# Layer 1's gates and branch projections with tokens on the output partitions and 512 moving weight columns

## The chip, the cores and the metric

One core of a Trainium2 chip runs the kernel. The engines named below are TensorE (PE in the profile; its weight loads are PEld), VectorE (DVE), ScalarE (ACT), GpSimd (POOL) and SyncE (SP, which issues the DMAs of the weights). The metric is the device time of one execution in microseconds; lower is better.

## The reference, cut to what matters

Two layers of a diffusion backbone work on 256 latent tokens and 256 context tokens with 1024 channels. Each layer projects the normalised tokens `h` once; three mixers (latent attention "mla", grouped attention "gqa", a Fourier mixing "four") work side by side. Their outputs, 512 wide each, are projected to 1024 channels, gated and summed, and the sum goes through one more projection:

```python
proj = h @ lp["w_in"]
o_mla = blocked_attend(q_mla, ..., MLA_QK ** -0.5)
o_gqa = blocked_attend(q_gqa, ..., GQA_DIM ** -0.5)
o_four = fourier_mix(proj[..., FOUR_START:GATE_START])
...
g_mla, g_gqa, g_four = jnp.split(jax.nn.sigmoid(gate_cols), N_BRANCH, axis=-1)
y = (g_mla * (o_mla.reshape(b, l, MLA_HEADS * MLA_V) @ lp["w_br_mla"])
     + g_gqa * (o_gqa.reshape(b, l, GQA_HEADS * GQA_DIM) @ lp["w_br_gqa"])
     + g_four * (o_four @ lp["w_four"]))
return y @ lp["w_o"]
```

Here `gate_cols` are the last 3 x 1024 columns of `proj`. A gated feed-forward layer with a short convolution follows. In the second layer (layer 1, `last` in the kernel) only the 256 latent tokens go on behind the keys and values.

## The kernel before

All data are 32 bit floats. A product of two such matrices is made of three matmuls on numbers split into a high and a low part: `mm3` (line 108) adds hi·hi, hi·lo and lo·hi (lines 109, 110 and 111 in the profile). `split` (line 120) makes the parts: ACT writes the high one (line 123, or 125 with a scale), DVE the low one (129 or 131). Weights come by `wchunk` (line 80): one DMA of 512 KB on SP's queue fills a raw tile of 128 x 1024 (three buffers), which is split into one of three high and one of three low buffers.

Activations lie channel major: a tile has 128 channels on the partitions and the tokens along the free side (256 in layer 1, `TQ`). `hs` are the eight normalised tiles of `h` (tags H0 to H7), `os` the four tiles of one mixer's output. `fm_group` (line 413) multiplies weights by them: a 128x128 block of the weight is stationary, the 256 tokens move, and the output has channels on the partitions. Two blocks of 128 output channels share one PSUM bank of 512 columns.

`merge` (line 579) makes, for one branch, two functions. `gate(mc)` takes 256 gate columns of `w_in` (two chunks of 4 k x 256), runs 2 x 8 x 3 = 48 matmuls of 256 columns and lets ACT write tanh of half the result, 128x512 (line 595). `branch(mc)` takes 256 columns of the branch weight (one chunk), runs 2 x 4 x 3 = 24 matmuls, and DVE multiplies the result by the gate plus one (602 for the first branch, straight into the sum `yT`; 604 for the others, whose result POOL adds to the sum, 605). There are three branches: 2 (four: `gF`, `bF`), 1 (gqa: `gG`, `bG`) and 0 (mla: `gM`, `bM`), each with `mc` from 0 to 3. The sum `yT` holds eight channel-major pieces in two tiles (tags Y0, Y1).

Where these run in layer 1: the list `fillers` gives one item behind each head of the gqa loop (lines 890 to 907): `gF` and `bF` of one mc behind each of heads 0 to 3, then the mla key and query tokens, then `gG(0)` and `gG(1)`. `bG(0)` and `gG(2)` stand between the two loops. The list `plan` gives the items behind the eight heads of the mla loop (945 to 960): `bG(1)`, `bG(2)`, `gG(3)`, `bG(3)`, then `gM(0)` to `gM(3)`. `heads_kq` (928) transposes one head's keys into the one bank of tag "tk" and its queries into a bank of tag "mm", a head ahead. Behind the loop stand the four `bM`, in banks of "s" and "mm" by turns, then the split of the eight pieces of the sum (line 972, tiles `yh` in H0 to H7), and the output projection `o` (lines 993 to 1016), with the first two chunks of 256 columns in two halves of k: 0 to 5, then 6 and 7.

PSUM has banks of tags "mm" (2), "s" (2, the scores of attention), "pt" (2, transposed probabilities), "o" (1) and "tk" (1). The order of the instructions on each engine is set at build time by a scheduler that takes the program's order as priority and a model of the times; within it, a filler's matmuls slip in between those of the heads.

## Time and profile before

| | us |
|---|---|
| median of 3 runs | 1373.64 (1371.73 to 1374.29) |
| the profiled execution, its own time | 1373.26 |
| its span in the profile | 1371.5 |
| PE busy in it | 1334.1 (97%) |
| DVE, ACT, POOL busy | 949.2, 660.1, 335.0 |

The profile is of one execution. Its span runs from the first to the last instruction; the execution's own time holds 1.8 us more. Layer 1's three mixers with gates and branches lie between about 955 us and 1145 us of the span: the gqa loop until about 1018, the hand-over with the mla keys and queries until about 1057, the mla loop until about 1126, and then the last branch, the sum and the start of the output projection. The shown durations of matmuls overlap, as they are pipelined and their ends are modelled; how fast they follow one another is read from their starts in the timeline.

### The profile page before, as it was taken

To read this page: it belongs to the slowest core of one execution; us is meant where nothing else is said; L and a number is where in the kernel's file an instruction comes from. 1 tells how busy PE (TensorE), PEld (TensorE's weight loads), DVE (VectorE), ACT (ScalarE), POOL (GpSimd) and SP (SyncE) were. 2 spreads that over 40 slices of the span, in tenths; PEclk is the share of its full clock that TensorE was granted. 3 is DMA by queue.
4 is the path that set the end of the run, shared out by engine and by line. 5 is a ranking of instruction groups with operands and counts; after the bars stand their busy time and mean duration, and the time that the engine had idled before them with its cause. 6 is when DMAs were issued, how large, how long until landed. Compare 5 with 4: busy or idle time off the path is not lost.

```text
span 1371.5 us, 22227 instructions
## 1 busy us (share of the span) xinstructions
PE 1334.1 (97%) x8381; PEld 1168.4 (85%) x8381; DVE 949.2 (69%) x1686; ACT 660.1 (48%) x1166; POOL 335.0 (24%) x399
## 2 busy tenths in 40 slices
PE   7999999999999899999999999999998999999998
PEld 4887888877888788888788888898988999899998
DVE  4675665676656647777876776777788867888853
ACT  4434555434556235434213443455665664666642
POOL 2211222365322421011000111222244524112200
PEclk8999999999999999999999999999999999999999
DMA  9733452243323524334674445634424366466663
GB/s 322 255 95 117 131 168 62 62 113 102 104 73 110 202 69 132 120 111 138 185 234 130 142 146 182 194 108 120 128 74 146 93 187 204 138 182 184 186 188 119
DMA packets 160437, 197.40 MB, mean 144 GB/s; under 512 B 7080, under 2 KB 144858, under 8 KB 160330
## 3 DMA queue, kind: packets, MB, share of 16 engines
q1 hardware_dynamic: 159328, 195.32, 46.1%
q8 instruction: 66, 1.08, 0.3%
q0 software_dynamic: 864, 0.61, 0.3%
q14 instruction: 41, 0.34, 0.1%
q10 hardware_dynamic: 138, 0.04, 0.0%
HBM read 191.76 MB, written 3.15 MB: 142 GB/s over the span
## 4 chain that ended last, share of the span: by engine, by line
PE 89%; DVE 6%; DMA 2%; POOL 1%; issue 1%; ACT 1%; SPq 0%; ACTq 0%; DVEq 0%; POOLq 0%
PE L0upp L109 6%; PE L0upp L110 6%; PE L0upp L111 6%; PE L1upp L109 3%; PE L1upp L110 3%; PE L1upp L111 3%; PE L0dp L109 3%; PE L0dp L111 3%; PE L0dp L110 3%; PE L0gp L109 3%; PE L0gp L111 3%; PE L0gp L110 3%; PE L1dp L111 2%; PE L1dp L110 2%; PE L1dp L109 2%; PE L0bp L111 1%
## 5 line engine op out<-in xcount | busy, mean ns | idle before, releaser
L109 PE MATMUL L0upp<-L0n_h,L0up_h 128*128 128x512 f32 (+1 forms) x384 | 141.5, 372 | 1.1 <-ACT L0n_h L377 1.1
L110 PE MATMUL L0upp<-L0n_h,L0up_h 128*128 128x512 f32 (+1 forms) x384 | 142.5, 373 | 0.0
L111 PE MATMUL L0upp<-L0n_h,L0up_l 128*128 128x512 f32 (+1 forms) x384 | 139.1, 371 | 0.0
L1079 POOL TENSOR_TENSOR L0sg<-L0sg,L0u 128x512 f32<-128x512 f32 x22 | 29.6, 1345 | 274.1 <-DVE L0u L1056 274.1
L109 PE MATMUL L1upp<-L1n_h,L1up_h 128*128 128x256 f32 x352 | 95.4, 283 | 1.1 <-ACT L1n_h L377 1.1
L111 PE MATMUL L1upp<-L1n_h,L1up_l 128*128 128x256 f32 x352 | 96.1, 283 | 0.0
L110 PE MATMUL L1upp<-L1n_h,L1up_h 128*128 128x256 f32 x352 | 95.8, 283 | 0.0
L109 PEld LDWEIGHTS L0upp<-L0n_h,L0up_h 128*128 128x128 f32 x384 | 71.9, 188 | 14.3 <-ACT L0n_h L377 1.5
L110 PEld LDWEIGHTS L0upp<-L0n_h,L0up_h 128*128 128x128 f32 x384 | 72.2, 188 | 13.0 <-DVE L0n_t L376 0.4
L111 PEld LDWEIGHTS L0upp<-L0n_h,L0up_l 128*128 128x128 f32 x384 | 72.2, 188 | 12.5
L123 ACT CAST L0up_h<-L0up_w 128x1024 fp32r<-128x1024 f32 x44 | 46.4, 1054 | 74.6 <-PE L0upp L110 51.2
L129 DVE TENSOR_TENSOR L0up_l<-L0up_w,L0up_h 128x1024 fp32r<-128x1024 f32 x44 | 59.2, 1348 | 32.1 <-ACT L0up_h L123 31.6
L109 PE MATMUL L0gp<-L0n_h,L0g_h 128*128 128x512 f32 x192 | 75.9, 396 | 1.1 <-ACT L0gt L594 1.1
L110 PE MATMUL L0gp<-L0n_h,L0g_h 128*128 128x512 f32 x192 | 75.7, 394 | 0.0
L111 PE MATMUL L0gp<-L0n_h,L0g_l 128*128 128x512 f32 x192 | 75.1, 396 | 0.1
L299 DVE SCALAR_TENSOR_TENSOR mod_acc<-mod_w,cpad,mod_acc 128x1024 f32<-128x1024 f32 x49 | 62.4, 1297 | 15.8 <-DMA mod_w<-in_w_mod_dram 15.8
L109 PE MATMUL L0dp<-L0act,L0dn_h 128*128 128x512 f32 (+1 forms) x196 | 72.8, 372 | 0.0
L111 PE MATMUL L0dp<-L0act,L0dn_l 128*128 128x512 f32 (+1 forms) x196 | 72.4, 370 | 0.0
L110 PE MATMUL L0dp<-L0act,L0dn_h 128*128 128x512 f32 (+1 forms) x196 | 72.2, 368 | 0.0
L109 PEld LDWEIGHTS L1upp<-L1n_h,L1up_h 128*128 128x128 f32 x352 | 65.9, 192 | 1.5 <-ACT L1n_h L377 1.5
L111 PEld LDWEIGHTS L1upp<-L1n_h,L1up_l 128*128 128x128 f32 x352 | 66.4, 192 | 0.0
L110 PEld LDWEIGHTS L1upp<-L1n_h,L1up_h 128*128 128x128 f32 x352 | 66.2, 192 | 0.1
(1564 smaller groups left out, 4265.2 us busy)
## 6 DMA issues: line engine op xcount, KB each, us to landing
mod_w<-in_w_mod_dram SPq DMA_DIRECT2D x96, 512.0 KB, 5.0
L0up_w<-in_w_up_dram SPq DMA_DIRECT2D x44, 512.0 KB, 3.6
L1up_w<-in_w_up_dram SPq DMA_DIRECT2D x44, 512.0 KB, 4.3
L0g_w<-in_w_in_dram SPq DMA_DIRECT2D x24, 512.0 KB, 3.7
L1g_w<-in_w_in_dram SPq DMA_DIRECT2D x24, 512.0 KB, 3.7
L0dn_w<-in_w_down_dram SPq DMA_DIRECT2D x20, 512.0 KB, 4.0
L1dn_w<-in_w_down_dram SPq DMA_DIRECT2D x16, 512.0 KB, 3.6
L0wo_w<-in_w_o_dram SPq DMA_DIRECT2D x8, 512.0 KB, 3.4
```

What stands on the lines that cost most here:

```text
L109: nc.tensor.matmul(ps, lh, rh, start=start, stop=False)
L110: nc.tensor.matmul(ps, lh, rl, start=False, stop=False)
L111: last_mm[0] = nc.tensor.matmul(ps, ll, rh, start=False, stop=stop).ins
L123: nc.scalar.copy(hi, src)
L129: ins = nc.vector.tensor_sub(lo, src, f(hi))
L299: nc.vector.scalar_tensor_tensor(acc, raw, cv, acc, op0=ALU.mult, op1=ALU.add)
L1079: nc.gpsimd.tensor_mul(g[:, :TQ], g[:, :TQ], us[1][:, :TQ])
```

## The change

In layer 1, `merge` returns the two functions of a new `merge_tokens`. Stationary is now a block of 128 tokens of `hs` or `os` (the high or the low part), and 512 columns of the weight move over it; the output has tokens on the partitions and one of two halves c of the channels along the free side. Both token tiles (tt) of a half have a PSUM bank of 512 columns each. A gate half takes four chunks of 2 k x 512 and 8 x 2 x 3 = 48 matmuls; it can be made in parts of one or two chunks, the banks being held between them. A branch half takes two chunks and 24 matmuls. Layer 0 keeps its `merge`.

The sum is kept token major, 128 x 1024 for each token tile. The adds of branch 0 go from POOL to DVE. `turn_sum(c)` transposes half c of the sum into four channel-major pieces in banks of tag "pt", and splits two pieces at a time (tiles in H4 to H7). The first half is turned between the two chunks of the last branch half, the second in the output projection, whose halves of k are now 0 to 3 and 4 to 7. The lists change: `fillers` have `gF(0)`, `bF(0)`, `gF(1)`, `bF(1)`, the key and query tokens, and `gG(0)` in two parts; `bG(0)` uses the "s" banks; a half of `gG(1)` stands ahead of the mla loop; `plan` has the other half of `gG(1)`, `bG(1)`, and `gM(0)` in parts of 1, 2, 1 chunks and `gM(1)` in parts of 2, 1, 1. The queries of an mla head are transposed into the "tk" bank, as the keys are.

```diff
--- before.py
+++ after.py
@@ -467,8 +467,7 @@
         run_after(mods["n1"], before)
         if last:
 
-            ytiles = [S.tile([P, 4, 256], F32, tag=f"Y{i}", name=f"{n_}y{i}") for i in range(2)]
-            yT = [ytiles[m // 4][:, m % 4, :] for m in range(KD)]
+            ytiles = [S.tile([P, D], F32, tag=f"Y{i}", name=f"{n_}y{i}") for i in range(2)]
             xk = [S.tile([P, 4, 256], F32, tag=f"Y{2 + i}", name=f"{n_}xk{i}") for i in range(2)]
             for m in range(KD):
                 nc.sync.dma_start(out=xk[m // 4][:, m % 4, :], in_=xT[m][:, :256])
@@ -576,14 +575,62 @@
             rope_apply(nc.vector, qg[tt], qg[tt], "qg", tt, H, 64, f"{n_}qgr{tt}")
 
 
+        def merge_tokens(b, wname, os, first):
+
+
+            begun, gates = {}, {}
+
+            def products(ps, w, xs, k0, nk):
+                for tt in range(2):
+                    ts = slice(tt * P, (tt + 1) * P)
+                    for k in (k0, k0 + 1):
+                        wh, wl = w(k - k0, 0, 512)
+                        mm3(ps[tt], xs[k][:, 0, ts], xs[k][:, 1, ts], wh, wl, k == 0, k == nk - 1)
+
+            def gate(c, n=4, tag=None):
+                i0, pss = begun.get(c) or (0, [pm(f"{n_}gp{b}{c}{tt}") for tt in range(2)])
+                for i in range(i0, i0 + n):
+                    w = wchunk(w_in, 2 * i, 2, GATE_START + b * D + c * 512, 512, f"{n_}g{b}{c}{i}")
+                    products(pss, w, hs, 2 * i, KD)
+                begun[c] = i0 + n, pss
+                if i0 + n < 4:
+                    return
+                if tag:
+                    t = S.tile([P, 2, 512], F32, tag=tag, name=f"{n_}gt{b}{c}")
+                    gates[c] = [t[:, tt] for tt in range(2)]
+                else:
+                    gates[c] = [S.tile([P, 512], F32, tag="gate", name=f"{n_}gt{b}{c}{tt}", bufs=3) for tt in range(2)]
+                for tt in range(2):
+                    nc.scalar.activation(gates[c][tt], pss[tt], AF.Tanh, scale=0.5)
+
+            def branch(c, pieces=(0, 1), bank="mm", own=None):
+                if pieces[0] == 0:
+                    begun[c] = 4, [pm(f"{n_}bp{b}{c}{tt}", bank) for tt in range(2)]
+                pss = begun[c][1]
+                for i in pieces:
+                    w = wchunk(a[wname][l], 2 * i, 2, c * 512, 512, f"{n_}b{b}{c}{i}", own)
+                    products(pss, w, os, 2 * i, 4)
+                if pieces[-1] == 0:
+                    return
+                for tt in range(2):
+                    y, g = ytiles[tt][:, c * 512:(c + 1) * 512], gates[c][tt]
+                    if first:
+                        nc.vector.scalar_tensor_tensor(y, g, 1.0, pss[tt], op0=ALU.add, op1=ALU.mult)
+                    else:
+                        nc.vector.scalar_tensor_tensor(g, g, 1.0, pss[tt], op0=ALU.add, op1=ALU.mult)
+                        (nc.gpsimd if b else nc.vector).tensor_add(y, y, g)
+            return gate, branch
+
         def merge(b, wname, os, first, bank="mm"):
+            if last:
+                return merge_tokens(b, wname, os, first)
             gates, packed = {}, {}
 
             def gate(mc, tag=None, halves=(0, 1)):
                 if 0 in halves:
-                    if tag or last:
-                        pool, nb = (wpool, 2) if tag == "mraw" else (S, None if tag else 3)
-                        t = pool.tile([P, 512 if not tag else 1024], F32, tag=tag or "gate", name=f"{n_}gt{b}{mc}", bufs=nb)
+                    if tag:
+                        pool, nb = (wpool, 2) if tag == "mraw" else (S, None)
+                        t = pool.tile([P, 1024], F32, tag=tag, name=f"{n_}gt{b}{mc}", bufs=nb)
                         packed[mc] = t[:, :2 * TQ]
                         gates[mc] = [t[:, i * TQ:(i + 1) * TQ] for i in range(2)]
                     else:
@@ -844,8 +891,8 @@
 
         if last:
             latents()
-            fillers = [[lambda mc=mc: gF(mc), lambda mc=mc: bF(mc)] for mc in range(4)]
-            fillers += [[kv_tokens], [q_tokens], [lambda: gG(0)], [lambda: gG(1)]]
+            fillers = [[lambda c=c, g=g: g(c)] for c in range(2) for g in (gF, bF)]
+            fillers += [[kv_tokens], [q_tokens], [lambda: gG(0, 2)], [lambda: gG(0, 2)]]
         else:
             fillers = [[lambda mc=mc, g=g: g(mc)] for mc in range(4) for g in (gF, bF)]
         fillers = [mods["g"][i:i + 1] + x for i, x in enumerate(fillers)]
@@ -916,10 +963,12 @@
         ktok, qtok, VM = L["ktok"], L["qtok"], L["VM"]
 
         gM, bM = merge(0, "w_br_mla", om, False, "s")
-        bG(0)
         if last:
-            plan = [[(bG, 1)], [(bG, 2)], [(gG, 3)], [(bG, 3)], [(gM, 0)], [(gM, 1)], [(gM, 2)], [(gM, 3, "D4")], []]
+            bG(0, bank="s")
+            plan = [[(gG, 1, 2)], [(bG, 1)], [(gM, 0, 1)], [(gM, 0, 2)], [(gM, 0, 1)], [(gM, 1, 2)], [(gM, 1, 1)],
+                    [(gM, 1, 1, "D4")], []]
         else:
+            bG(0)
             plan = [[(bG, 1)], [(gG, 2), (bG, 2)], [(gG, 3), (bG, 3)], [],
                     [(gM, 1, "X3")], [(gM, 2, "mraw")], [(gM, 3, "mraw")], [], [(gM, 0)]]
         plan = [[lambda x=x: x[0](*x[1:]) for x in xs] for xs in plan]
@@ -932,14 +981,14 @@
                 nc.tensor.transpose(tk[:96, tt * P:(tt + 1) * P], ktok[tt][:, h, :], ident)
             k2 = pair(f"D{h % 2}", f"{nm}k")
             split(tk[:96, :], k2[:96, 0, :], k2[:96, 1, :], p["gk"])
-            tq = pm(f"{nm}tq", "mm" if last else "tk")
+            tq = pm(f"{nm}tq", "tk")
             for tt in range(NTQ):
                 nc.tensor.transpose(tq[:96, tt * P:(tt + 1) * P], qtok[tt][:, h, :], ident)
             q2 = pair(f"D{2 + h % 2}", f"{nm}q")
             split(tq[:96, :TQ], q2[:96, 0, :TQ], q2[:96, 1, :TQ], p["gq"])
             return k2, q2
 
-        gG(2 if last else 1)
+        gG(1, 2) if last else gG(1)
         with tc.issue_after(last_mm[0]):
             kq = heads_kq(0)
         for h in range(H):
@@ -959,19 +1008,35 @@
                 om.append(finish_pair(of, h // 2, 1, f"{nm}om"))
             run(mods["m"][h:h + 1] + plan[h])
         run(plan[8])
-        for mc in range(4):
-            bM(mc, ("s", "mm", "pt", "s")[mc] if not last else ("s", "mm")[mc % 2],
-               [("H0", "H1")] if mc == 3 and not last else None)
-
-        cw = conv_params(l)
-
-
         ys = []
-        for m in range(KD):
-            y = pair(f"H{m}" if last else f"{'BD'[m // 4]}{m % 4}", f"{n_}yh{m}")
-            split(yT[m], y[:, 0, :TQ], y[:, 1, :TQ], 0.5)
-            ys.append(y)
-        if not last:
+
+        def turn_sum(c):
+
+            for j in range(2):
+                ps = pm(f"{n_}yt{c}{j}", "pt")
+                for i in range(2):
+                    m = 4 * c + 2 * j + i
+                    for tt in range(2):
+                        nc.tensor.transpose(ps[:, i * 256 + tt * P:i * 256 + (tt + 1) * P], ytiles[tt][:, m * P:(m + 1) * P], ident)
+                y = pair(f"H{4 + 2 * c + j}", f"{n_}yh{c}{j}")
+                split(ps, y[:, 0, :], y[:, 1, :], 0.5)
+                ys.extend(y[:, :, i * 256:(i + 1) * 256] for i in range(2))
+
+
+        if last:
+            bM(0, bank="s")
+            bM(1, (0,))
+            turn_sum(0)
+            bM(1, (1,))
+            cw = conv_params(l)
+        else:
+            for mc in range(4):
+                bM(mc, ("s", "mm", "pt", "s")[mc], [("H0", "H1")] if mc == 3 else None)
+            cw = conv_params(l)
+            for m in range(KD):
+                y = pair(f"{'BD'[m // 4]}{m % 4}", f"{n_}yh{m}")
+                split(yT[m], y[:, 0, :], y[:, 1, :], 0.5)
+                ys.append(y)
             xt = [S.tile([P, 2, 512], F32, tag=f"X{i}", name=f"{n_}x{i}") for i in range(4)]
             xn = [xt[m // 2][:, m % 2, :] for m in range(KD)]
             for m in range(KD):
@@ -995,8 +1060,11 @@
             wos.append(wchunk(a["w_o"][l], 0, KD, mc * 256, 256, f"{n_}wo{mc}",
                               None if last else ([("H2", "H3"), ("H4", "H5")], [("H6", "H7"), None])[mc]))
             pos.append([pm(f"{n_}o{mc}_{i}", ("mm", "s")[mc]) for i in range(2)])
-        for ks in (range(6), range(6, KD)):
+        k1 = 4 if last else 6
+        for ks in (range(k1), range(k1, KD)):
             for mc in range(2):
+                if last and ks[0] == 0 and mc == 1:
+                    turn_sum(1)
                 for k in ks:
                     for i in range(2):
                         wh, wl = wos[mc](k, i * P, P)
```

## Rows read from the trace of the kernel before

**Rows 1.** The page: busy time by engine; the chain that ended last, by engine.

```profile
PE 1334.1 (97%) x8381; PEld 1168.4 (85%) x8381; DVE 949.2 (69%) x1686; ACT 660.1 (48%) x1166; POOL 335.0 (24%) x399
...
PE 89%; DVE 6%; DMA 2%; POOL 1%; issue 1%; ACT 1%; SPq 0%; ACTq 0%; DVEq 0%; POOLq 0%
```

**Rows 2.** Busy time in two stretches: by engine; clock, DMA share, GB/s.

```profile
1018.00:1057.00 39.00, 34.46 (x245) 31.34 (x243) 34.05 (x68) 22.12 (x39) 20.87 (x24) 1.00 0.47 135
...
1057.00:1126.00 69.00, 68.48 (x535) 65.75 (x536) 51.84 (x89) 45.63 (x90) 25.97 (x23) 1.00 0.47 138
```

**Rows 3.** Layer 1's gate products: durations ns, first and last start.

```profile
L109 PE MATMUL L1gp<-L1n_h,L1g_h x192: 277/283/387, 955.9 to 1125.0; 128*128 128x256 f32 x192
```

**Rows 4.** The timeline of PE, gate products: start us, shown duration us.

```profile
962.03 0.28 PE L110 MATMUL L1gp<-L1n_h,L1g_h 128*128 128x256 f32 x1
...
963.23 0.28 PE L111 MATMUL L1gp<-L1n_h,L1g_l 128*128 128x256 f32 x1
```

**Rows 5.** The timeline of PE: the Fourier projection's start and end.

```profile
916.52 0.40 PE L109 MATMUL L1fp<-L1fo_h,L1n_h 128*128 128x512 f32 x1
...
927.43 0.28 PE L109 MATMUL L1A<-dft1d,L1f 128*128 128x256 f32 x1
```

**Rows 6.** The timeline of PE: scores of mla head 3, values of head 2.

```profile
1082.48 0.39 PE L110 MATMUL L1m3s<-L1m3k,L1m3q 96*128 96x512 f32 x1
...
1083.41 0.39 PE L111 MATMUL L1m3s<-L1m3k,L1m3q 96*128 96x512 f32 x1
...
1083.99 0.36 PE L693 MATMUL L1m2o<-L1m2ph,L1VM 128*128 128x256 f32 x1
```

**Rows 7.** The timeline of PE: four transposes in the mla loop.

```profile
1081.00 0.60 PE L684 MATMUL L1m2pt<-ident,L1m2p 128*128 128x128 f32 x4
...
1081.56 0.28 PE L111 MATMUL L1gp<-L1n_h,L1g_l 128*128 128x256 f32 x1
```

**Rows 8.** Evictions of gates and branches, the adds, the small low parts.

```profile
L595 ACT ACTIVATE L1gt<-L1gp x12: 589/598/602, 964.4 to 1127.0; 128x512 f32<-128x512 f32 x12
...
L604 DVE SCALAR_TENSOR_TENSOR L1gt<-L1gt,L1bp x8: 668/674/689, 1061.7 to 1144.4; 128x512 f32<-128x512 f32 x8
...
L605 POOL TENSOR_TENSOR L1y<-L1y,L1gt x8: 1281/1348/2367, 1062.5 to 1145.2; 128x512 f32<-128x512 f32 x8
...
L131 DVE SCALAR_TENSOR_TENSOR L1yh<-L1y,L1yh x8: 406/411/1510, 1139.2 to 1148.6; 128x256 fp32r<-128x256 f32 x8
```

**Rows 9.** Low parts on DVE of 128x512 and of a weight chunk.

```profile
L129 DVE TENSOR_TENSOR L1m7ph<-L1m7pt,L1m7ph x2: 681/682/684, 1128.1 to 1128.7; 128x512 fp32r<-128x512 f32 x2
...
L129 DVE TENSOR_TENSOR L1wo_l<-L1wo_w,L1wo_h x8: 1210/1226/2301, 1138.0 to 1160.5; 128x1024 fp32r<-128x1024 f32 x8
```

**Rows 10.** The timeline of PE at the end of the stage.

```profile
1131.92 0.62 PE L109 MATMUL L1bp<-L1m5om,L1b_h 128*128 128x256 f32 x3 [1.35 <-ACT L1m5om L713]
...
1140.42 0.36 PE L109 MATMUL L1o<-L1yh,L1wo_h 128*128 128x256 f32 x1
...
1145.36 0.28 PE L110 MATMUL L1o<-L1yh,L1wo_h 128*128 128x256 f32 x1
```

**Rows 11.** The last mla head: its scores; its output's high and low part.

```profile
L111 PE MATMUL L1m7s<-L1m7k,L1m7q x2: 397/439/481, 1117.3 to 1118.3; 96*128 96x512 f32 x2
...
1131.46 0.40 ACT L713 CAST L1m5om<-L1m6of 128x256 fp32r<-128x256 f32 x1 [0.49 <-DVE L1m6of L698]
...
1131.89 0.43 DVE L714 TENSOR_TENSOR L1m5om<-L1m6of,L1m5om 128x256 fp32r<-128x256 f32 x1 [0.47 <-ACT L1m5om L713]
```

**Rows 12.** Waits of PE from 955 to 1145 us: total, times, longest.

```profile
PE L1gp L109 <- ACT L1gt L595: 0.8, 1, 0.8
...
PE L1m0s L109 <- ACT L1m0q L125: 1.0, 1, 1.0
```

**Rows 13.** The timeline at the first mla head: queries, the key's low part.

```profile
1056.15 0.40 PE L937 MATMUL L1m0tq<-ident,L1qtok 128*96 128x128 f32 x2
...
1057.11 0.74 DVE L131 SCALAR_TENSOR_TENSOR L1m0k<-L1m0tk,gk,L1m0k 96x512 fp32r<-96x512 f32 x1
```

## The prediction

> **What bounds the kernel now.** I read the page first: TensorE (PE) is busy 97% of the 1371.5 us span, and the chain that ended last runs over PE for 89% of it [rows 1]. So a change counts mostly by the time that it takes out of PE's stream, plus what it does to the places where PE stands. Then I read the stretch that the change touches, about 955 to 1145 us, by windows: at the two attention loops PE is nearly solid (68.48 of 69 us between 1057 and 1126), while between 1018 and 1057 it is busy 34.46 of 39 us with VectorE (DVE) busy 34.05; TensorE's granted clock is 1.00 in both, the 2.4 GHz level [rows 2]. So two thirds of the stretch is PE bound, and the hand-over from one attention to the other is held by DVE and ScalarE (ACT) in part.
>
> Busy time hides the rate of the matmuls, as their shown durations overlap (283 ns each for 256 columns, [rows 3]). The rate is the distance from start to start, in the timeline. Gate products of 256 columns start every 0.120 us: from 962.03 to 963.23 there are ten steps [rows 4]. The only place in layer 1 that already works like the changed code (stationary tokens, 512 moving weight columns) is the Fourier projection: 48 matmuls from 916.52 to the start of the next kind at 927.43, 10.91 us or 0.2273 us each [rows 5]. Two of 256 columns cost 0.240, one of 512 costs 0.2273: each instruction carries some 13 ns beside its columns. That 13 ns is what the change is after.
>
> **The change part by part.** *The products.* Before: 12 gates of 48 matmuls and 12 branch blocks of 24, so 864 of 256 columns (each of the three gate lines has 192, [rows 3]); 864 x 0.120 = 103.7 us. After: 6 gates of 8 k x 2 token tiles x 3 = 48, and 6 branches of 24, so 432 of 512 columns; 432 x 0.2273 = 98.2 us. Saved: 5.5 us. The bound on the worse side is the slowest row of 512 columns, the scores of the second attention, with four steps in 0.93 us, 0.2325 each [rows 6]: 100.4 us, 3.3 saved. No row of 512 columns is faster than the Fourier ones, so 5.5 is the better end too.
>
> The Trainium skill, "TensorE: Matmul & The Clock Gate", section "Back-to-back issue gap", gives a gap of N/2.4 + 2.5 ns, which speaks against this change: 109.2 and 215.8 ns, so an estimate of 1.1 us saved, not 5.5. The timeline shows 120 and 227 [rows 4, 5], a fixed part about five times as large; the sum goes by the rows.
>
> The weight loads fall from 864 to 432 too, and the same skill ("Perfetto Trace Analysis", section "Identifying the Most-Contended Engine") judges TensorE's headroom by the busy share of the loads, 85% here [rows 1]. By that one would hope for more: 432 loads at 1168.4 / 8381 = 0.139 us are 60 us. But the two steps differ by 107 ns for 256 columns, just the columns' own time at 2.4 GHz; so the loads lie under the columns, and only the 13 ns are to be had.
>
> *Transposes added.* 16 of 128x128, in four groups of four. Four such in the attention run from 1081.00, and the second matmul behind them starts at 1081.56: 0.56 less the one normal step of 0.12 is 0.44 us a group [rows 7]. 4 x 0.44 = 1.8 us on PE; from 1.3 (the shown 0.60 less the 0.28 of one matmul) to 2.2 (all of the 0.56).
>
> *Evictions, splits and loads.* Gate tanh: 12 of 128x512 before and after, 598 ns each. Branch eviction on DVE: 12 of 128x512 both times, 674 to 688 ns. The splits of weight chunks are 24 + 12 both times (a chunk is 2 k x 512 in place of 4 k x 256), and so are the loads in SP's queue, with rows twice as long in DRAM; hidden under the products, as now: costed at nothing. The adds of the second attention's branch leave POOL (1348 ns each, four of them) for DVE; the trace has no such add on DVE, so I bound it by the lo of 128x512 (682 ns) and by the 128x1024 lo (1226 ns) and take the first, which has its size [rows 8, 9]. The eight small splits of the sum (0.41 us on each of ACT and DVE) become four of 128x512 from PSUM, 0.6 and 0.68: 0.6 us less on each.
>
> *The end of the stage.* Now PE waits 1.35 us for the last attention output, and then the output projection starts in a stutter: 18 matmuls take from 1140.42 to 1145.36, 4.94 us where 18 x 0.120 = 2.2, so 2.8 us are lost to halves of the sum that are not split yet [rows 10]. After the change, from the moment t at which the last output is there: branch half 0 lacks one k (6 matmuls, 1.4 us), then two evictions (1.4) and two adds (1.4) on DVE, four transposes (0.44), ACT's hi (0.6), DVE's lo (0.68), with hops of 0.03 (ACT's 1131.46 + 0.40 to DVE's 1131.89, [rows 11]) and PE's latency twice (0.28 shown less 0.12 of step, 0.16): the output projection can run from about t + 6.3. Cover on PE: 1.4 us of half 0, 2.7 of half 1, 0.9 of transposes, 5.0 in all. A hole of 1.3 us, against 2.8 before. Later DVE owes 2.8 for half 1, 1.4 for two lo, and four weight splits of 1.23; PE has 48 x 0.120 = 5.8 us of first-half products before it needs the second half, so I see no second hole. Change: -1.5 us, from -2.8 (no hole) to +2 (weight splits queued ahead on DVE). The 1.35 us ahead of t [rows 10] I leave as it is: the chain from the last head's last score (1118.3) to its lo (1131.9 + 0.43) took 14 us [rows 11], and the work that can lie beside it (two quarter gates 5.4, three k of half 0 4.1, two k of half 1 2.7, the head's own 1.9) is 14.1.
>
> *Banks.* A channel-major group sat in one PSUM bank and the next group took the other. A token-major group holds both "mm" banks until its tanh or its eviction is done, so PE cannot start the next group meanwhile. It is covered by the stagger: token tile 0 ends six matmuls (1.36 us) ahead of tile 1, and the 0.60 us tanh fits into that; the branch's 0.67 on DVE fits less surely. The nearest row is PE's wait for a gate's tanh, 0.8 us once [rows 12]. With some ten hand-overs I take one such wait, +1.0; from nothing to +4 (half of them). One quarter-gate pair (1.6 us more PE work than before) moves ahead of the second attention, where PE has 4.5 us idle [rows 2]; if it falls into those gaps, 1.6 us more is gained, which I leave to the lower end.
>
> *The q transposes* of each head move from an "mm" bank to the single "tk" bank, behind the k transposes: they now wait until DVE has read k's bank. What is queued behind them on PE are that head's scores, which ACT and DVE then wait for. At the first head q was transposed at 1056.15, while k's bank was read until 1057.11 + 0.74 [rows 13]: up to 1.7 us later, and PE waits there already (1.0 us for q, [rows 12]). From 0 to +1.7; I take +0.5, as half a gate's products stand ready beside it. In the loop k and q are made a head ahead, so it costs nothing there.
>
> *Sum*: -5.5 + 1.8 - 1.5 + 1.0 + 0.5 = -3.7 us. The profiled run took 1373.26 us (span 1371.5), 0.4 under the median of 1373.64 and inside the runs' spread; 1373.26 - 3.7 = **1369.6 us**.
>
> **Rivals.** (a) *The holes close*: larger pieces of work stand ready for PE, so the hole ahead of the output projection goes (-1.3 more), the moved quarter gates fill the hand-over (-1.6) and the q term is nothing (-0.5): 1366.2. For it: PE's idle 4.5 us; against: it is DVE that is busy there. (b) *The pairs of banks eat it*: +4 in place of +1.0, 1372.6. For it: 0.8 us rows exist; against: the stagger. (c) *Slower, by short fillers*: heads 2, 4, 6 and 7 of the second attention now have a quarter gate each, 2.7 us, where most had a whole group of 5.8. Then a head's own 4.0 us on PE (scores 1.4, eight transposes 0.9, eight products with the values 1.0, k and q 0.7) plus 2.7 is 6.7 us, while the chain of its max, exp, POOL product, transposes, split and products took 14 us for the last head [rows 11]; 8.4 us if six tenths of that is its own work and the rest queues, an estimate. If heads ran strictly one behind the other, PE would stand 1.7 us in each of the four, and as long again ahead of t, where the 1.35 us would double: +6.8 + 1.4, 1377.8. It decides when a head overlaps the next by less than 1.7 us. Against it: the scores of head 3 start over 1.5 us ahead of head 2's products with the values (1082.48 and 1083.99, [rows 6]), and the transposes of later heads lie earlier still. (d) *The change doesn't do what it says*: in the loops, with the other engines' traffic beside it, a product of 512 columns takes nearly as long as two of 256, as the scores' 0.2325 goes half the way to [rows 6]; 1.1 us saved in place of 5.5, 1374.0. The Fourier rows stand against it [rows 5]. (The gap rule of the page named above would end at the same time.)
>
> **How the numbers follow.** Forecast 0.47 (1367.7 to 1371.7), (a) 0.15, (b) 0.22, (c) 0.13, (d) 0.03. A measurement of this kernel can tell about 0.2% from no change, 2.7 us: faster means under 1370.9, slower over 1376.4. Four fifths of the forecast's own range lies under 1370.9 (0.38), with (a) 0.53 for faster; the rest of the forecast with (b) and (d), 0.34, is the same; (c), 0.13, is slower. The unknowns alone reach from 1364.7 (-5.5 + 1.3 - 2.8 - 1.6) to 1379.9 (-3.3 + 2.2 + 2 + 4 + 1.7); the range 1365.0 to 1375.5 leaves out (c) and a thin part of (a).
>
> **What the profile after would show.** Steps of 0.227 us for gates and branches of layer 1 (right), or 0.232 and more (the size is off). Four transposes a group at 0.44 us, with PE's idle time ahead of the output projection near 1.3 us in one piece. Waits of PE for gate tanh or branch evictions at more than two hand-overs would show (b); repeated waits of 1.5 us for a head's exp, split or q in the second attention (c). Wrong altogether would be a stretch from the Fourier stage to the feed-forward that is as long as before with steps of 0.227: then work moved into DVE's queue sets the length.

## The result and the profile after

The changed kernel takes 1386.67 us (median of 5 runs, 1386.27 to 1387.02), the kernel before 1373.64 (5 runs, 1371.73 to 1374.87): a ratio of 1.0098, 95% interval 1.0085 to 1.0112. That is 13.0 us slower, where 1369.6 was forecast and 1375.5 was the upper end of the range. The profiled execution (1386.27) has a span of 1384.5 us, again 13.0 more.

The page of the changed kernel, busy time and chain:

```profile
PE 1338.2 (97%) x7965; PEld 1151.2 (83%) x7965; DVE 947.2 (68%) x1686; ACT 658.7 (48%) x1162; POOL 328.5 (24%) x395
...
PE 86%; DVE 6%; DMA 3%; ACT 2%; POOL 2%; issue 1%; SPq 0%; DVEq 0%; ACTq 0%; POOLq 0%
```

Beside [rows 1], PE has 416 matmuls fewer (432 products less, 16 transposes more) and still 4 us more of busy time. The busy share is 97% both times, so it doesn't show the loss.

The lines of the changed kernel (duration ns min/median/max, first and last start), and after "..." the first feed-forward products:

```profile
L109 PE MATMUL L1gp<-L1g_h,L1n_h x96: 387/389/486, 956.2 to 1098.6; 128*128 128x512 f32 x96
...
L1020 PE MATMUL L1yt<-ident,L1y x16: 272/273/421, 1146.3 to 1158.3; 128*128 128x128 f32 x16
...
L621 DVE TENSOR_TENSOR L1y<-L1y,L1gt x4: 679/680/682, 1145.5 to 1150.9; 128x512 f32<-128x512 f32 x4
...
L109 PE MATMUL L1upp<-L1n_h,L1up_h x352: 278/283/415, 1186.3 to 1314.4; 128*128 128x256 f32 x176
```

The same feed-forward line of the kernel before:

```profile
L109 PE MATMUL L1upp<-L1n_h,L1up_h x352: 274/283/387, 1174.8 to 1301.4; 128*128 128x256 f32 x176
```

From the first gate product to the first feed-forward product ("the stage" from here on) the kernel before takes 1174.8 - 955.9 = 218.9 us [rows 3], the changed one 1186.3 - 956.2 = 230.1: 11.2 of the 13.0 us are lost there. And the last gate product starts at 1099, where it was 1125: gate work ran out 41 us before the last attention step, where it used to last nearly to its end.

The windows of the changed kernel (us; PE, PEld, DVE, ACT, POOL busy; granted clock, DMA share, GB/s):

```profile
1018.00:1057.00 39.00, 36.34 (x181) 30.27 (x179) 33.74 (x63) 21.54 (x34) 21.35 (x24) 1.00 0.52 162
1057.00:1126.00 69.00, 64.46 (x337) 52.68 (x338) 50.26 (x81) 43.32 (x83) 22.59 (x19) 0.98 0.39 118
...
1100.00:1108.00 8.00, 5.66 (x32) 4.40 (x31) 5.78 (x11) 5.28 (x12) 1.30 (x2) 1.00 0.42 133
1108.00:1115.00 7.00, 6.36 (x30) 4.82 (x30) 3.93 (x9) 3.63 (x9) 1.41 (x2) 0.76 0.00 0
1115.00:1141.00 26.00, 21.80 (x124) 17.13 (x122) 15.78 (x32) 14.97 (x33) 9.90 (x12) 1.00 0.36 118
1141.00:1150.00 9.00, 5.08 (x26) 3.75 (x26) 6.56 (x11) 3.48 (x5) 1.02 (x2) 1.00 0.73 256
1150.00:1157.00 7.00, 4.92 (x24) 4.76 (x24) 3.25 (x7) 0.60 (x1) 0.00 (x0) 0.52 0.46 150
...
1185.00:1192.00 7.00, 5.89 (x34) 5.58 (x34) 5.86 (x14) 4.52 (x10) 0.74 (x1) 0.76 0.00 0
```

The hand-over became fuller (36.34 of 39 us against 34.46 in [rows 2]), as rival (a) had it. Behind 1100 it is the opposite. The kernel before was solid there at first:

```profile
1100.00:1108.00 8.00, 8.00 (x68) 7.99 (x67) 4.99 (x9) 5.25 (x11) 2.27 (x3) 1.00 0.34 96
```

In the changed kernel PE stands 2.3 us of the first 8, 4.2 of the 26 behind 1115, 3.9 of the 9 behind 1141. And the granted clock, 1.00 all through this stage in the kernel before, falls three times: 0.76 of 7 us, 0.52 of 7 us, 0.76 of 7 us. In shorter windows these are stretches of 3.4, 6.8 and 3.4 us at 0.50, the 1.2 GHz level. Ahead of each PE had stood a good part of the time (5.66 us busy of 8, 5.08 of 9, and 5.38 of 7.5 ahead of the third).

So the account of the stage is: products -5.0 and transposes +1.8 (below); PE's idle time, summed over its gaps, 18.4 us against 10.4, so +8.0; clock 0.24 x 7 + 0.48 x 7 = +5.1, an estimate that takes PE to be the limit while the clock is low. Together that is +9.9 of the 11.2; the other 1.3 us has no place in it. The third clock stretch, 1.7 us, lies in the feed-forward, behind the stage.

Waits of PE in the changed kernel from 1060 to 1182 us (total, times, longest):

```profile
PE L1yt L1020 <- DVE L1y L621: 2.6, 2, 1.3
PE L1o L110 <- DVE L1yh L131: 2.1, 1, 2.1
PE L1bp L109 <- ACT L1m5om L760: 2.0, 2, 1.4
PE L1m4tq L986 <- DVE L1m3st L727: 1.1, 1, 1.1
PE L1m7tq L986 <- DVE L1m6st L727: 1.1, 1, 1.1
PE L1m4s L109 <- ACT L1m4q L125: 0.7, 1, 0.7
```

Two things are on this list that the waits of the kernel before don't have: the q transposes of later heads (L986) wait for DVE, and the transposes of the sum wait twice for an add. The wait for a low part of the sum is 2.1 us in one piece, where the kernel before has two shorter ones:

```profile
PE L1o L110 <- DVE L1yh L131: 1.5, 2, 1.1
```

Nothing waits for a gate's tanh, here or earlier in the stage. The timeline of the changed kernel at head 4 shows the first:

```profile
1103.60 0.60 PE L981 MATMUL L1m4tk<-ident,L1ktok 128*96 128x128 f32 x4
...
1104.54 1.29 DVE L724 TENSOR_REDUCE L1m3st<-L1m3s 128x1 f32<-128x512 f32 x2 [0.59 <-PE L1m3s L111]
...
1105.75 0.74 DVE L131 SCALAR_TENSOR_TENSOR L1m4k<-L1m4tk,gk,L1m4k 96x512 fp32r<-96x512 f32 x1
...
1106.63 0.39 PE L986 MATMUL L1m4tq<-ident,L1qtok 128*96 128x128 f32 x2 [1.13 <-DVE L1m3st L727]
...
1107.71 0.50 PE L109 MATMUL L1m4s<-L1m4k,L1m4q 96*128 96x512 f32 x1 [0.69 <-ACT L1m4q L125]
```

The keys of head 4 are transposed at 1103.60, but DVE's order, set at build time, has the two maxima of head 3 first (1104.54 + 1.29), and DVE reads the keys' bank from 1105.75 to 1106.49. Only then may q go into the same bank: PE stands 1.13 us, then 0.69 more for q's high part, 1.8 us in all ahead of the scores that DVE and ACT need next. (The profile names DVE's last reciprocal as the releaser; what PE needs is the read of the bank that ended at 1106.49.)

### The profile page after: what moved, and what is told of

Its sections match the earlier page's. It is cut to its first block, busy times and chain, and to the rows that moved or that the text cites. A ratio compares the mean times of both kernels' runs of the same rounds, so it can differ in the third digit from the quotient of the medians.

```text
span 1384.5 us, 21368 instructions
## 1 busy us (share of the span) xinstructions
PE 1338.2 (97%) x7965; PEld 1151.2 (83%) x7965; DVE 947.2 (68%) x1686; ACT 658.7 (48%) x1162; POOL 328.5 (24%) x395
## 3 DMA queue, kind: packets, MB, share of 16 engines
q8 instruction: 63, 1.03, 0.3%
## 4 chain that ended last, share of the span: by engine, by line
PE 86%; DVE 6%; DMA 3%; ACT 2%; POOL 2%; issue 1%; SPq 0%; DVEq 0%; ACTq 0%; POOLq 0%
PE L0upp L109 6%; PE L0upp L110 6%; PE L0upp L111 6%; PE L1upp L109 3%; PE L1upp L110 3%; PE L1upp L111 3%; PE L0gp L109 3%; PE L0gp L111 3%; PE L0gp L110 3%; PE L0dp L109 2%; PE L0dp L111 2%; PE L0dp L110 2%; PE L1dp L111 2%; PE L1dp L109 2%; PE L1dp L110 2%; PE L0bp L111 1%
## 5 line engine op out<-in xcount | busy, mean ns | idle before, releaser
L111 PE MATMUL L0upp<-L0n_h,L0up_l 128*128 128x512 f32 (+1 forms) x384 | 139.1, 371 | 0.0
L111 PE MATMUL L1upp<-L1n_h,L1up_l 128*128 128x256 f32 x352 | 97.1, 285 | 0.0
L111 PEld LDWEIGHTS L0upp<-L0n_h,L0up_l 128*128 128x128 f32 x384 | 72.2, 188 | 12.5
L129 DVE TENSOR_TENSOR L0up_l<-L0up_w,L0up_h 128x1024 fp32r<-128x1024 f32 x44 | 59.2, 1347 | 32.1 <-ACT L0up_h L123 31.5
L111 PE MATMUL L0gp<-L0n_h,L0g_l 128*128 128x512 f32 x192 | 75.1, 396 | 0.0
L111 PE MATMUL L0dp<-L0act,L0dn_l 128*128 128x512 f32 (+1 forms) x196 | 72.4, 369 | 0.0
L111 PEld LDWEIGHTS L1upp<-L1n_h,L1up_l 128*128 128x128 f32 x352 | 67.3, 194 | 0.0
```

Of the source, the lines that this page charges most:

```text
L111: last_mm[0] = nc.tensor.matmul(ps, ll, rh, start=False, stop=stop).ins
L129: ins = nc.vector.tensor_sub(lo, src, f(hi))
```

## The experiments

For each: the median (lowest to highest), the ratio to the runs of the kernel before on the same chip (whose medians were 1373.3 to 1374.0), and from its profile the stage, the time from the last gate product to the last attention step ("bare"), and the time lost at the lower clock ("clock": one less the granted clock, summed over windows of 3.5 us from 950 to 1195). The last three columns are of one execution each. All that lies ahead of the stage has the same source in all these kernels, and yet the stage starts between 951.7 us (e3_no_turn) and 958.5 us (e6_before_tk) in the profiled executions. Single executions differ by such amounts for reasons that the edits don't touch, so a difference of two medians is read beside that of the stage.

| kernel | us | ratio (95%) | stage | bare | clock |
|---|---|---|---|---|---|
| before | 1373.64 | | 218.9 | 4.6 | 0 |
| after | 1386.67 | 1.0098 (1.0085 to 1.0112) | 230.1 | 41.2 | 6.8 |
| e2_tq_pt | 1379.24 (1376.67 to 1380.58) | 1.0037 (1.0024 to 1.0050) | 225.6 | 31.9 | 6.8 |
| e6_before_tk | 1385.52 (1384.74 to 1387.03) | 1.0081 (1.0063 to 1.0100) | 227.9 | 20.1 | 1.7 |
| e10_before_tk_pin | 1380.21 (1378.71 to 1381.99) | 1.0048 (1.0032 to 1.0065) | 225.9 | 5.1 | 1.7 |
| e11_before_pt | 1376.66 (1372.68 to 1379.55) | 1.0021 (1.0010 to 1.0032) | 222.1 | 11.4 | 0 |
| e4_early_gates | 1379.84 (1377.88 to 1380.38) | 1.0039 (1.0026 to 1.0052) | 223.6 | 20.1 | 0 |
| e7_before_tk_early | 1390.46 (1389.39 to 1390.75) | 1.0115 (1.0097 to 1.0132) | 233.7 | 28.5 | 5.1 |
| e1_pin | 1385.09 (1383.55 to 1388.68) | 1.0082 (1.0057 to 1.0107) | 231.2 | 11.2 | 8.5 |
| e5_pin_pt | 1382.62 (1381.32 to 1383.79) | 1.0059 (1.0040 to 1.0078) | 226.0 | 11.2 | 6.9 |
| e3_no_turn | 1384.23 (1379.74 to 1385.53) | 1.0068 (1.0046 to 1.0090) | 229.6 | 41.7 | 6.8 |
| e8_tail | 1376.09 (1372.97 to 1377.81) | 1.0016 (1.0005 to 1.0028) | 220.9 | 31.5 | 3.4 |
| e9_spread | 1381.26 (1373.99 to 1383.80) | 1.0048 (1.0032 to 1.0064) | 225.2 | 9.2 | 6.9 |
| e12_fill | 1376.98 (1374.96 to 1379.71) | 1.0026 (1.0016 to 1.0036) | 221.4 | 8.7 | 3.4 |

### The bank of the queries

*e2_tq_pt*, the changed kernel with q in another bank:

```diff
-            tq = pm(f"{nm}tq", "tk")
+            tq = pm(f"{nm}tq", "pt" if last else "tk")
```

> Changed kernel, with the q transposes of the mla heads in a bank of tag pt in place of tk. Theory B (the one tk bank holds up the heads): waits of 1.13, 1.06, 0.69 and 0.61 us for q and its bank go, 3 to 5 us, about 1382 to 1384. Theory A (no filler left): same within 2 us, as the chain of a head stays as long; it may also lose, as pt is taken from the probabilities.

It came out at 1379.24, 7.4 us faster than the changed kernel, more than theory B's 3 to 5; the stage is 4.5 us shorter. Its waits of PE from 1060 to 1182 hold none for tq any more; the first two are those of the stage's end:

```profile
PE L1yt L1020 <- DVE L1y L621: 2.3, 2, 1.6
PE L1o L110 <- DVE L1yh L131: 1.5, 1, 1.5
```

By the medians the bank is over half of the loss, and the mla loop (first scores to last attention step) falls from 75.2 to 68.3 us.

*e6_before_tk*, the kernel before with only this edit of the change:

```diff
-            tq = pm(f"{nm}tq", "mm" if last else "tk")
+            tq = pm(f"{nm}tq", "tk")
```

> The kernel before with one thing of the change: the q transposes of the second attention go to the bank tk, where those of k are. Everything else stays channel major. Theory of the prediction (k and q are made a head ahead, so the shared bank costs nothing where gate steps lie between): 1373.5 to 1374.5 us. Theory 'the bank puts q behind VectorE's split of k, and so behind the maxima of the head before, whatever the layout': 4 to 7 us more, 1377 to 1381 us, with waits of TensorE for tq of the heads 1 to 7. The theory that the bank hurts only where gate steps have run out says 1373.5 to 1375.5 us, since they last to 1125 us here.

It took 1385.52, a loss of 11.7 us, more than any theory said (by the stage 9.0). With not one product turned round, a loss nearly as large as that of the whole change is there; the layout isn't needed for it. But its profile lists few waits for tq; the largest from 1035 to 1190:

```profile
PE L1m5pt L684 <- POOL L1m5p L681: 2.4, 1, 2.4
PE L1o L110 <- DVE L1yh L131: 2.2, 2, 1.9
...
PE L1m7tq L937 <- DVE L1m7k L131: 0.6, 1, 0.6
PE L1m0tq L937 <- DVE L1m0k L131: 0.6, 1, 0.6
```

The timeline of PE and DVE in this kernel, at the first head, shows why:

```profile
1057.78 2.34 DVE L129 TENSOR_TENSOR L1b_l<-L1b_w,L1b_h 128x1024 fp32r<-128x1024 f32 x2
...
1059.03 0.38 PE L109 MATMUL L1bp<-L1g1og,L1b_h 128*128 128x256 f32 x1
...
1060.05 0.73 DVE L131 SCALAR_TENSOR_TENSOR L1m0k<-L1m0tk,gk,L1m0k 96x512 fp32r<-96x512 f32 x1
...
1060.93 0.39 PE L937 MATMUL L1m0tq<-ident,L1qtok 128*96 128x128 f32 x2 [0.57 <-DVE L1m0k L131]
```

Where q must wait for the bank, the order of work made at build time puts branch and gate products ahead of it (here from 1059.03; in the kernel before q came without them, at 1056.15 [rows 13]). The wait is filled, so hardly any row shows it. But the scores come later (those of head 7 start 68.8 us behind those of head 0, against 59.2 in the kernel before), more gate work is spent on the early heads, and it is gone by 1120 where it lasted to 1125 although the loop now ends 10 us later: "bare" is 20.1 us against 4.6. The first head that stands bare shows the 2.4 us.

*e10_before_tk_pin* holds the gate steps in place, with the bank still shared:

```diff
-            run(mods["m"][h:h + 1] + plan[h])
+            with tc.issue_after(last_mm[0]) if last and h else nullcontext():
+                run(mods["m"][h:h + 1] + plan[h])
```

> The kernel before, channel major, with the q transposes in the bank tk (1385.5 us), and the planned gate steps of head 1 and later held behind that head's own scores, so that they can't be drawn forward into the waits that the bank makes. Theory 'the bank costs by the order of the work: each q that waits draws gate steps forward, and the last heads stand bare': most of the 11.7 us comes back, 1375.5 to 1379 us, and gate products last to 1125 us or later. Theory 'the bank costs by itself, since k and q of a head and k of the next take turns behind VectorE's queue': 1382 to 1387 us, with waits for tq or tk in most heads.

1380.21 lies between the two forecasts: with "bare" at 5.1, 5.3 us come back by the medians, about half. By the stage it is 2.0 of 9.0. The rest stays, and now the bank's waits stand in the open:

```profile
PE L1m1tq L937 <- DVE L1m1k L131: 2.0, 1, 2.0
...
PE L1m4s L109 <- ACT L1m4q L125: 0.9, 1, 0.9
```

So the shared bank costs both by itself and by the gate work that is drawn forward to hide it. How the loss divides is open: the two measures differ, and no run held the gate steps in the kernel before without the shared bank, so what the holding itself costs is still in the second part.

*e11_before_pt* puts q into "pt" in the kernel before:

```diff
-            tq = pm(f"{nm}tq", "mm" if last else "tk")
+            tq = pm(f"{nm}tq", "pt" if last else "tk")
```

> The kernel before, channel major, with the q transposes in the bank pt, which they share with the transposes of the probabilities, in place of a gate's bank. Theory 'only the bank of k is costly, since q then waits for the split of its own head's k': 1373 to 1375.5 us. Theory 'any bank that attention uses ties q to VectorE's queue': 1377 to 1382 us. If gates were short of a bank before, it is faster: 1371 to 1373 us.

It took 1376.66, 2.7 us above the kernel before: a little over the first theory's range and under the second's. Sharing with the probabilities costs a quarter of what sharing with the keys does, but isn't free. So the bank that e2_tq_pt uses is no free one either, and its 7.4 us is the difference of two shared banks; a gate's bank, which the channel-major kernel lends to q, is held through a whole gate half in the new layout.

The Trainium skill, "Perfetto Trace Analysis", section "Matmuls", says that independent groups should rotate through different PSUM banks, so that their evacuation overlaps the next group's work. The runs e2_tq_pt and e6_before_tk agree with it, at 7.4 and 11.7 us for one pair of groups in each of eight heads.

### Gate work that runs out

*e4_early_gates*, the kernel before, channel major, with its planned items all behind heads 0 to 3:

```diff
-            plan = [[(bG, 1)], [(bG, 2)], [(gG, 3)], [(bG, 3)], [(gM, 0)], [(gM, 1)], [(gM, 2)], [(gM, 3, "D4")], []]
+            plan = [[(bG, 1), (gG, 3)], [(bG, 2), (bG, 3)], [(gM, 0), (gM, 1)], [(gM, 2), (gM, 3, "D4")], [], [], [], [], []]
```

> Kernel before (channel major, 1373.64 us), with the list of the mla loop bunched: the last gqa gate, both gqa branches and all four mla gates stand behind heads 0 to 3, nothing behind heads 4 to 7. Theory A (it is the bunching, not the layout): slower by 5 to 9 us, 1379 to 1383, with waits of PE in heads 4 to 7 and a stretch at half clock. If the layout itself (banks held in pairs, longer products) is what costs: within 2 us of 1373.64.

It took 1379.84, 6.4 us above the kernel before. That is theory A's time, but without its signs: the clock doesn't fall in the stage, and no wait of PE in heads 4 to 7 is over 0.4 us. PE's idle time in the stage rises by 2.0 us only (12.4 against 10.4), while the stage is 4.7 us longer; how the rest arises is open. Work, banks and layout are those of before; only the place of the gate work differs ("bare" 20.1).

*e7_before_tk_early* has this edit and that of e6_before_tk together, still channel major.

> The kernel before, channel major, with the two suspected side effects of the change alone: q transposes in the bank tk, and the gate steps planned into the first four heads. If the side effects make up the loss and add up as apart (6.4 us for the early gates, 7.4 us for the bank as measured in the changed kernel): 1386 to 1388 us, the changed kernel's own time, and the last filler product at about 1115 us with waits for k and q behind it. If the bank's wait and the bare heads are the same loss: 1380 to 1382 us. If token major steps themselves are needed for the loss: within 1 us of the early gates alone, 1379 to 1381 us.

It took 1390.46, 16.6 us above the kernel before and over every forecast. The two are neither the same loss nor quite a sum (11.7 + 6.4 = 18.1). Two side effects of the change, put into the old layout, cost more than the whole change did.

*e1_pin* goes the other way: the changed kernel with each head's gate steps held behind its own scores.

```diff
-            run(mods["m"][h:h + 1] + plan[h])
+            with tc.issue_after(last_mm[0]) if last else nullcontext():
+                run(mods["m"][h:h + 1] + plan[h])
```

> Changed kernel (1386.67 us), with each item of the mla loop's list tied behind the scores of the head that it stands behind, so that quarter gates cannot run ahead. Theory A (gates run early, their last product at 1099.0, and heads 3 to 7 are left uncovered: 13.6 us of late steps between 1100 and 1140): most of that comes back, some 7 to 10 us, 1377 to 1380, and the half-clock stretch at 1109 goes. Theory B (the q transposes in the one tk bank make the heads wait, whatever stands beside them): under 3 us, 1384 or more. Theory C (the turn of the sum at the end costs it) expects no change in this stretch and 5 us of late steps to stay behind the loop in either case.

It took 1385.09, 1.6 us less than the changed kernel, with intervals that overlap and a stage that is 1.1 us longer, so no gain is shown; of the forecasts only theory B's has this time. "Bare" fell from 41.2 to 11.2 us, but the hand-over lost what it had been given: its largest wait is now 3.6 us at 1053, for an add that ends the first attention's last head, and a clock stretch of 6.8 us follows it. *e5_pin_pt* has this edit and that of e2_tq_pt together.

> The changed kernel with both edits: the gate steps of each second-attention head held behind that head's own scores, and the q transposes in the bank pt, so that they no longer wait for the split of k. Theory 'two independent losses': the gains of the single edits add, 7.4 us (bank) and 1.6 us (holding), so 1386.7 - 9.0 = 1377.7 us, and the waits of TensorE for the m-heads' k and q fall under 0.3 us each in every head. Theory 'one loss seen twice' (the bank's wait only shows where no gate step covers it, so either edit takes the same time): 1379 to 1380 us, no better than the bank edit alone. Theory 'the hand-over is the price of holding' (a hole of 3.6 us opens where the first attention ends when gate steps are held back): 1380 to 1383 us, slower than the bank edit alone, with that hole of 3 us or more seen near 1053 us.

It took 1382.62, slower than e2_tq_pt without the holding by 3.4 us. The third theory gave the time, but not the place: in the hand-over its waits are 1.8 us for a low part, 1.6 for the query tokens and 1.1 for an output, and no single hole of 3; the stage's end cost it 3.6 us in waits for the adds. So holding all gate steps back doesn't pay.

### The end of the stage

In the changed kernel's timeline the end reads:

```profile
1141.90 0.50 PE L109 MATMUL L1bp<-L1b_h,L1m5om 128*128 128x512 f32 x1 [1.35 <-ACT L1m5om L760]
...
1143.85 1.07 PE L111 MATMUL L1bp<-L1b_h,L1m5om 128*128 128x512 f32 x4
1144.28 1.28 DVE L620 SCALAR_TENSOR_TENSOR L1gt<-L1gt,L1bp 128x512 f32<-128x512 f32 x2 [1.97 <-PE L1bp L111]
...
1146.31 0.41 PE L1020 MATMUL L1yt<-ident,L1y 128*128 128x128 f32 x2 [1.31 <-DVE L1y L621]
...
1148.02 0.88 PE L1020 MATMUL L1yt<-ident,L1y 128*128 128x128 f32 x6 [1.30 <-DVE L1y L621]
...
1151.51 0.68 DVE L131 SCALAR_TENSOR_TENSOR L1yh<-L1yt,L1yh 128x512 fp32r<-128x512 f32 x1
...
1152.24 0.58 PE L110 MATMUL L1o<-L1yh,L1wo_h 128*128 128x256 f32 x1 [2.08 <-DVE L1yh L131]
```

All four groups of the last branch end together: their last products (L111, four at 1143.85) stand at the end of the block. Then DVE has the evictions of both halves, all four adds and two weight splits ahead of the first half's low part (1151.51). PE's holes are 1.31, 1.30, 0.41 (for DVE's copy of the convolution's weights) and 2.08: 5.1 us, where 1.3 was forecast and the same view of the kernel before has 1.5. From 1149.9 on the clock is at 0.50.

*e3_no_turn* leaves the 16 transposes out (the splits read the untransposed sum, so the output projection works on the wrong layout):

```diff
-                        nc.tensor.transpose(ps[:, i * 256 + tt * P:i * 256 + (tt + 1) * P], ytiles[tt][:, m * P:(m + 1) * P], ident)
```

> Changed kernel without the 16 transposes of the sum: the split takes the token-major halves as they lie (so the output projection works on a wrong layout; that part of the computation is left out). Theory C (the chain through evictions, adds, transposes and split at the end costs it): the stretch from the last attention output to the end of the output projection loses the 1.8 us of transposes and much of its 10 us of late steps, 4 to 6 us in all, 1381 to 1383. Theory A alone: only the transposes' own time, about 2 us, 1384.5.

It took 1384.23, 2.4 us less than the changed kernel, near the forecast 1.8 us of transposes; the two intervals overlap, and the stage is only 0.5 us shorter. The output projection still waits 2.07 and 2.04 us for the sum's parts, and between them PE waits 1.49 us for DVE's copy of the convolution's weights. So the transposes aren't what the end waits for; all three waits are for parts that ACT and DVE make.

*e8_tail* puts that queue in another order, with q in "pt" as in e2_tq_pt: the second half's last piece goes behind the first half's last product, and the second half's evictions and the later weight splits behind the first half's low parts:

```diff
+            end0 = last_mm[0]
...
-            bM(1, (1,))
+            first_lo[0] = marks["split"]
+            with tc.issue_after(end0):
+                bM(1, (1,), ev=first_lo[0])
```

> The changed kernel with the q transposes in pt and the end of the stage put in another order: the last products of the second half of the sum are held behind the last product of the first half, and VectorE's second-half evictions and weight splits behind the first half's low parts. Theory 'the queue of VectorE at the end sets the holes' (all four groups end together, then four products, adds and splits stand ahead of the first half's low part): TensorE's holes ahead of the output projection fall from 3.8 to 5.1 us to 1.5 to 2.5, and the time from 1379.2 to 1375.5 to 1377.5 us. Theory 'the holes only move' (the second half's evictions are now late by what the first gained): 1378.5 to 1380 us. Worse is possible where the weight split, now later, holds the projection: above 1380 us, with a wait for a weight's low part ahead of the first step of the projection.

It took 1376.09, as the first theory had it, 3.2 us under e2_tq_pt and the lowest median of the token-major kernels. Its timeline at the end (line numbers stand up to three higher in this kernel):

```profile
1135.09 1.03 PE L1023 MATMUL L1yt<-ident,L1y 128*128 128x128 f32 x8
...
1136.86 0.69 DVE L133 SCALAR_TENSOR_TENSOR L1yh<-L1yt,L1yh 128x512 fp32r<-128x512 f32 x1 [0.37 <-ACT L1yh L127]
1137.57 0.27 PE L76 MATMUL cw_p<-ident,cw_r 88*128 88x88 f32 x1 [1.37 <-DVE L1yh L133]
...
1139.37 0.56 PE L110 MATMUL L1o<-L1yh,L1wo_h 128*128 128x256 f32 x1 [1.03 <-DVE L1gt L623]
```

The adds follow their evictions, the eight transposes come in one block without a wait, and the holes are 1.37 and 1.03, in all 2.4 us against 3.8 in e2_tq_pt; the second one now ends with the second half's evictions (L623), which the edit put behind the low parts. The clock lost 3.4 us instead of 6.8, so the gain isn't the holes' alone.

*e9_spread* adds to e8_tail a spread of the gate and branch work in smaller pieces, those of head 1 and later held behind that head's scores:

```diff
-            plan = [[(gG, 1, 2)], [(bG, 1)], [(gM, 0, 1)], [(gM, 0, 2)], [(gM, 0, 1)], [(gM, 1, 2)], [(gM, 1, 1)],
-                    [(gM, 1, 1, "D4")], []]
+            plan = [[(gG, 1, 2), (bG, 1, (0,))], [(bG, 1, (1,))], [(gM, 0, 1)], [(gM, 0, 1)], [(gM, 0, 1)], [(gM, 0, 1), (gM, 1, 1)],
+                    [(gM, 1, 1)], [(gM, 1, 2, "D4")], []]
...
-            run(mods["m"][h:h + 1] + plan[h])
+            with tc.issue_after(last_mm[0]) if last and h >= 1 else nullcontext():
+                run(mods["m"][h:h + 1] + plan[h])
```

> The changed kernel with the bank pt, the other order at the end of the stage (both as in the run before it, 1376.1 us), and the gate steps spread: half a gate or half a branch for each head of the second attention, those of head 1 and later held behind that head's own scores, the two pieces ahead of them free for the hand-over. Theory 'gate steps used up too early are what is left' (heads 3 to 7 stand bare there, and TensorE's late steps between 1100 and 1130 us sum to 7.8 us against 1.5 in the kernel before): they fall to 2 to 3 us, and the time to 1370.5 to 1372.5 us, below the kernel before. Theory 'what is held back from the hand-over is paid there' (3.6 us when all were held): 1375 to 1379 us, with a hole of 2 us or more near 1050 us. Theory of the prediction's sum (steps -5.5, transposes +1.8, all else near level): 1369 to 1371 us.

*e12_fill* adds to e8_tail the holding for heads 5 to 7 alone, and puts the second half's first piece behind the last attention step, into the 1.35 us wait:

```diff
-            run(mods["m"][h:h + 1] + plan[h])
+            with tc.issue_after(last_mm[0]) if last and h >= 5 else nullcontext():
+                run(mods["m"][h:h + 1] + plan[h])
...
-            bM(1, (0,))
+            with tc.issue_after(last_o[0]):
+                bM(1, (0,))
```

> The changed kernel with the bank pt and the other order at the end of the stage (1376.1 us with these two), and two more edits of where gate and branch steps lie: only the gate steps of heads 5 to 7 are held behind their head's scores, so that heads 2 and 3 stand bare in place of 3 to 7, and the 12 products of the second half's first piece go behind the last step of attention, where TensorE waits 1.35 us for the last output's copy. Theory 'bare last heads are what is left, and the hand-over keeps its steps': the late steps from 1100 us to the projection fall from 10.5 us to 4 or 5, and the time to 1371 to 1373.5 us, at or below the kernel before. Theory 'held steps cost what they save' (as when all were spread): 1376 to 1381 us, with new waits for q's low parts ahead of the probabilities' transposes, or a stretch of TensorE at half clock after a hole of about 2 us.

They took 1381.26 and 1376.98: the first lost, over every forecast, and the second didn't gain. In e9_spread four heads now wait 0.3 to 0.6 us ahead of the probabilities' transposes for the next head's q, which shares their bank, the wait for the last output is 2.5 us, and the clock costs 6.9. In e12_fill most of the late waits went (0.9 us stayed in the last head), and the wait for the last output with them, but the outputs of heads 1 to 3 now wait 1.4, 0.3 and 1.0 us, in a stretch that has no gate step instead. Where the gate steps lie decides which heads wait; every order that was tried left some of them waiting.

No kernel was found that beats the kernel before.

## Why the prediction was wrong

*Products, -5.5: right.* Undisturbed steps of the changed kernel are 0.227 us (twelve from 982.78 to 985.50, 2.72 us). Over all steps that follow one of their kind without a wait the mean is 0.234, and 0.123 in the kernel before; 864 x 0.1229 - 432 x 0.2342 = 5.0 us. Rival (d) is out. The prediction's last sign of being wrong altogether came true: steps of 0.227 in a stretch that is no shorter than before.

*Transposes, +1.8, and adds on DVE: right.* Eight transposes of the sum in e8_tail take 1.03 us, and one alone is shown as 0.27; that is 0.11 a step, 1.7 for 16. e3_no_turn gives 2.4 within its noise, and the add took 0.680 us.

*Banks, +1.0, rival (b): not seen as a wait.* PE waits for no gate's tanh in the whole stage. Whether the pairs of banks cost something by the order of the work, as the q bank does, no run tested.

*The q transposes, +0.5: the step that failed.* "In the loop k and q are made a head ahead, so it costs nothing there." Being a head ahead fixes when q is needed, not when its bank comes free. The bank waits for DVE's read of k, and that stands in DVE's queue behind the maxima of the head before. The cost is 7.4 us in the changed kernel and 11.7 in the old layout, over eight heads (by the stage 4.5 and 9.0). [rows 13] held the mechanism: up to 1.7 us for one head. The term was to be taken for each head, and the gate work that fills such waits to be counted as spent.

*The end, -1.5: wrong in size and sign.* PE's waits there are 5.1 us against 1.5 before, so +3.6 and the clock behind them. The sum listed DVE's work but let the first half through alone. What stands in DVE's order is what counts: e8_tail, which makes the order that the prediction supposed, gains 3.2 us on e2_tq_pt. The bound of +2 for "weight splits queued ahead" had the right cause, though too small, and it wasn't the one taken.

*Rival (c)* had the direction and the cause, gate work too short for the heads, but laid it on four heads with a quarter gate each. In fact the scheduler uses all gate work up by 1099, ahead of the scores of head 3 (1101.63), and heads 3 to 7 have only branch products; e4_early_gates prices a bare stretch of 20.1 us, in the old layout, at 6.4 us by itself. The q bank isn't what uses it up so early here: with q in "pt" it still ends at 1102.0 (e2_tq_pt), while in the old layout it lasts to 1120.5 (e11_before_pt). What does, no run shows.

*The clock* had no term, since [rows 2] has it at 1.00. It fell behind places where PE stood, and took at most 6.8 us of the 13.0. Without it the loss would be about 6, and the time near the upper end of the unknowns' sum, 1379.9; that is an estimate, since no run kept the clock up in the changed kernel.

*What is left.* e8_tail, with both failed steps mended, is still 2.2 us above the kernel before, where the sum has it 3.7 below. The profile is of its fastest execution (1372.97 us, 0.3 under that of the kernel before), which began the stage 3.7 us earlier; the stage itself took 220.9 against 218.9 us. The account of it, with products and transposes as in the changed kernel, is: products -5.0, transposes +1.8, idle time 13.5 against 10.4, so +3.1, and +1.7 for the half of the clock's loss that lies in the stage, together +1.6 of the 2.0. Of the idle time 5.2 us lie in the bare heads, where PE is busy for 24.76 of 30 us between 1100 and 1130. That they can be had back isn't shown: e12_fill removed the late waits and got others.

```profile
1100.00:1130.00 30.00, 24.76 (x142) 19.95 (x140) 20.53 (x41) 18.57 (x42) 10.67 (x12) 1.00 0.42 134
1130.00:1139.50 9.50, 6.22 (x33) 5.08 (x33) 5.88 (x12) 3.49 (x5) 1.01 (x2) 1.00 0.69 241
1139.50:1143.00 3.50, 3.50 (x17) 3.50 (x18) 3.50 (x5) 0.00 (x0) 0.00 (x0) 0.52 0.17 47
```

(Windows of e8_tail: the bare heads, the end of the stage, and the clock's fall behind it.)

## What to carry to other kernels

When an edit moves a tile to another bank, ask who must read the tile that is in it, what stands ahead of that reader in its engine's queue, and take the wait once for every pass of the loop. Work that fills waits is a stock: a new wait that shows in no row may have been paid with work that a later pass needed, so look at when the filling work ends, not only at the waits. And a small gain in a nearly solid stretch is at risk of more than its size, since the clock can fall behind a hole.

## What the runs showed of the hardware

The granted clock falls to 0.50, the 1.2 GHz level, for 3.4, 6.8 or (once, in e2_tq_pt) 10.2 us, after stretches in which PE stood for a part (5.08 us busy of 9 ahead of the fall at 1150). Four transposes are then shown at 1.06 us instead of 0.60 [rows 7]:

```profile
1109.38 1.06 PE L981 MATMUL L1m5tk<-ident,L1ktok 128*96 128x128 f32 x4
```

and the output projection's products start every 0.21 us instead of 0.12. The same hole doesn't always bring it: a wait of 1.8 us in the hand-over stands in the profiles of all eight token-major kernels, and three of them (e3_no_turn, e5_pin_pt, e9_spread) have a fall there. What decides that is open. In the kernel before, e4_early_gates and e11_before_pt the clock didn't fall in this stage at all, though e4_early_gates was 6.4 us slower.
